# Second row tile normed first, stored values in their own pool, second half's sums in strips, short tile not last, idle flips ahead of the rows

## The chip, the cores and the metric

The kernel runs on one core of one Trainium2 chip. The metric is the device time of one execution in microseconds. Engines: TensorE (PE, its weight loads PEld), VectorE (DVE), ScalarE (ACT), GpSimd (POOL), and SyncE (SP), which issues nearly all DMAs from one queue in order.

## The reference

A two-layer encoder step, for a prompt of 2048 rows and a sample of 64 rows, model width 1024, 16 heads of 64. What matters here is the part ahead of each attention:

```
layer a: h = rms_norm(x, norm_a);  q, k, v, gate = split(h @ w_in_a, 4)
         band attention (own chunk of 64 and 8 before), * silu(gate), @ w_out_a, + x
shared:  h = rms_norm(x1, norm_kv); k, v = split(h @ w_kv, 2)
layer b: h = rms_norm(x1, norm_b);  q, gate = split(h @ w_in_b, 2)
         stick-breaking attention over k, v, * silu(gate), @ w_out_b, + x1
out:     rms_norm(x2, norm_f); k and v rows of both layers are outputs too
```

All in float32, with each product made of three products of high and low parts (h·h, h·l, l·h).

## The kernel before, in words

`projections` is called once per layer and does the part above. It has four stages, each for a half of the rows (half 0: rows 0 to 1023 and the 64 sample rows, half 1: rows 1024 to 2047):

1. **Values of half 0.** Row tiles of 128 are loaded (`fetched`), normed (`normed`: square on ACT, mean on DVE, power and scaling on POOL, or scaling on DVE where that is asked for), turned by eight 128x128 flips on PE (`turned`) and cut into high and low parts (`parted`, into x_own for half 0 and x_big for half 1). Then `values` makes v for one row tile and one half of the columns: 24 products on PE for a full tile, 16 for the sample tile (rows 2048 to 2111, tile 16). The weights of a column half come as four raw blocks (`block_rows`), cut into eight pairs vwh, vwl (`two_blocks`: ACT and DVE); the second column half's are written over the first's. `leave` evicts: a cuts v and stores it (vs), b copies it (vn), stores it twice, and puts off loading the row before each row (vps), a subtraction and a store (vs), by a count of ticks (`after`, `tick`). In b the last three tiles of the second column half leave their difference to staged work beside the pairs (`stage_diff`).
2. **Pairs of half 0.** The k, q and gate projections are made for two blocks of 128 columns at once by a Strassen-like scheme (`pair`): eight slots, each of 12 products into ps_x, ps_z or ps_y. Some products take sums and differences of quarters of the rows' forms (`mix`: one, two, three, for each of four column strips u) as moving operand (`mixed`), others differences of the weights (t1 to t4, made by `weights_of`: load, s1, s2 scale on POOL; b1, b2 cut whole forms; −t1 and so on subtract on POOL; t1 and so on cut). Slot 0 needs b1, then evicts to c on ACT and cuts t2; slot 1 needs t1 and the sums. Other work is staged beside the slots (`all_pairs`, `staging`).
3. **Values of half 1**, as 1. Its first tiles and weight blocks are prepared in the last pairs of half 0; the weight blocks of rows 512 and up lie in x_own, in the first four row groups and the columns below 512. The sums go to x_own too, which holds the forms of half 0 no more.
4. **Pairs of half 1** for the kinds that aren't left for the attention stage (8 pairs in a, 4 in b).

The order on each engine: while `order.on` is set, compute instructions stay in the order in which they are written; elsewhere a scheduler orders them by a simulated timeline. DMAs by `nc.sync` are ordered by it too, and SP issues them in order. Pools of tiles are stacked: a pool opened after another was closed takes its place in memory, and a tile's first writer waits for the accesses of what lay there. vs and vn were tiles of the values' pool (v0, v1), where the pairs' pool (st0, st1: t2 to t4, c, hl and others) comes next. After both layers' projections come their attention stages, which the change does not touch.

Of the kernel before, what the change touches and what calls it, by code (L numbers as in the profile page):

```python
# [44 lines left out]
RATE = dict(a=0.4, b=0.3)  # L45
LAG = dict(a=3, b=5)
# [78 lines left out]
def encoder_step(ctx: ExitStack, tc: tile.TileContext, a: dict, o: dict):  # L125
# [143 lines left out]
    def projections(L, x_of, begin, w_v, cv, gv, out_v, jobs, first, prompt, sample, stages):  # L269
        with ExitStack() as own, ExitStack() as beside, ExitStack() as early:  # L270
# [11 lines left out]

            def mixed(hf, i):

                if hf == 0 and i == 3:
                    return quarter(0, 0, 1)
                x, r = sums[hf][i // 2], 4 * (i % 2)
                return [lambda k, c=c: x[:, r + k, c : c + CH] for c in (0, CH)]

            def into(hf, i, u):  # L290
                if hf == 0 and i == 3:
                    return [x[:, :4, CH + u * P : CH + u * P + P] for x in xs[0]]
                x, r = sums[hf][i // 2], 4 * (i % 2)
                return [x[:, r : r + 4, c + u * P : c + u * P + P] for c in (0, CH)]
# [94 lines left out]
            waiting, flight, lagging, seqs = [], [], [], [[*range(NK), len(TOK) - 1], [*range(NK, 2 * NK)]]  # L389
# [15 lines left out]
            def values(hf, half, i, t, vws, pool, vps):  # L405
                r0, n = TOK[t]
# [22 lines left out]
                def leave():  # L429
# [17 lines left out]
                    if L == "a" or half and t in seqs[hf][-3:]:  # L447
                        return
# [74 lines left out]
            def pair(hf, kind, c0, hp, forms, pool, this, following, third, event):  # L523
# [9 lines left out]
                def plain(ps):  # L533
                    c = pool.tile([P, CH], F32, name="c", tag="c", bufs=CS[L])
                    act.activation(c, ps, AF.Copy)
                    return c
# [111 lines left out]
            def all_pairs(hf, todo, made, forms, pool, staging, events):  # L648

                for i, (kind, w, c0, g, hp) in enumerate(todo):  # L650

                    def event(p):
                        for x in events.get(i, {}).get(p, []):
                            x()
                        flight[:] = [x for x in flight if any(x[0] is y for y in waiting)]
                        left = max(8 * (staging["until"] - i) - p, 1)
                        staging["due"] += len(staging["todo"]) / left if staging["todo"] else 0
                        while staging["todo"] and staging["due"] >= 1:
                            tags, stage = staging["todo"][0]
                            if any(sum(tag in x[1] for x in flight) >= n for tag, n in tags.items()):  # L660
# [8 lines left out]
                    pair(hf, kind, c0, hp, forms, pool, made[i], following, third, event)  # L669
# [39 lines left out]
            with tc.tile_pool(name=f"v0_{L}", bufs=1) as pool:  # L709
# [17 lines left out]
                xt[1] = load(seq[1])  # L727
                tile1 = turned(seq[1], norm(seq[1], xt[1]))
# [7 lines left out]
                for i, t in enumerate(seq):  # L736
                    leave = values(0, 0, i, t, vws, pool, vps)
# [10 lines left out]
                    if i == len(seq) - 1:  # L748
                        vws = [x for j in range(4) for x in two_blocks(j, raw[j], vw(pool))]
                    leave()  # L750
                    if i >= 4:
                        mixing.pop(0)()
                    tick()
                for i, t in enumerate(seq):
                    values(0, 1, i, t, vws, pool, vps)()
# [7 lines left out]
                    if 4 <= i < 8:  # L763
                        split(*into(0, 3, i - 4), tmp[i].rearrange("p (k t) -> p k t", k=4))
# [24 lines left out]
            staging = dict(pool=spaces.__enter__(), todo=staged[0], until=last - 2, due=1.0)  # L789
# [41 lines left out]
            all_pairs(0, todo[0], made, forms, spool, staging, events)  # L831
# [6 lines left out]
            with tc.tile_pool(name=f"v1_{L}", bufs=1) as pool:  # L838
                vps = two_places() if L == "b" else None
                where = [(ahead, 2), (ahead, 2), (ahead, 2), (pool, 1), (ahead, 2), (ahead, 2), (pool, 1), (ahead, 2)]  # L840
                xt[3] = fetched(seq1[3], *where[3])
                for i, t in enumerate(seq1):
                    leave = values(1, 0, i, t, vws, pool, vps)
# [4 lines left out]
                    if i < 4 or L == "a" and i < 5:  # L848
                        values_beside(i, ("oh", "ol"))
                    if i == 5:  # L850
                        raw = [block_rows(1, j, ("xr", "xr", "oh", "oh")[j]) for j in range(4)]
                    if i == NK - 1:
                        vws = [x for j in range(4) for x in two_blocks(j, raw[j], vw(ahead if j < 2 else pool))]
                    leave()
                    if i + 3 < NK:
                        normed(seq1[i + 3], xt[i + 3], ahead)
                    if i == NK - 1:
# [4 lines left out]
                    tick()  # L862
                for i, t in enumerate(seq1):
                    values(1, 1, i, t, vws, pool, vps)()
                    for _ in range(1 + i % 2):
# [8 lines left out]
                    if i == 2:  # L874
                        run(made[0], "s1")
                    if i == 4:
# [8 lines left out]
                forms[1] = whole_forms("ol")  # L885
            early.close()
            spool = beside.enter_context(tc.tile_pool(name=f"st1_{L}", bufs=1))
# [5 lines left out]
            run(made[0], "b2", "-t2", "-t4")  # L893
            run(made[1], "load", "s1")
            all_pairs(1, todo[1], made, forms, spool, staging, {})
# [692 lines left out]
    new_diffs = [("new", t, 1) for t in (6, 7, 16, 13, 14, 15)]  # L1588
# [6 lines left out]
    staged_b = [new_diffs[0], keys_b[10], new_diffs[1], outs[0], new_diffs[2]]  # L1595
# [19 lines left out]
    with (  # L1615
# [173 lines left out]
        (beside_b, [staged_b, new_diffs[3:]]),  # L1789
# [287 lines left out]
```

## Time and profile before

| | us |
|---|---|
| median of 3 runs (lowest, highest) | 3258.44 (3257.12, 3260.55) |
| profiled execution, its own time | 3262.03 |
| its span, first to last instruction | 3260.2 |
| PE busy | 3142.9 (96%) |
| values of half 0 in a, first flips to the first pair | 7 to 125 |
| values of half 1 in a | 397 to 496 |
| values of half 0 in b | 1405 to 1525 |
| values of half 1 in b | 1808 to 1914 |

Of the granted clock, the mean over the span is 0.989 of full speed. In the timeline a row has start, duration, engine, line, operation, out<-in, sizes and count, and in brackets the idle time of the engine before it with its releaser. In the view by stretches a row has the stretch, its length, the busy time and count of PE, PEld, DVE, ACT and POOL, PE's granted clock, the DMA engines' share and GB/s. The chain of waits has start, duration and what. Line 114 is the helper through which every compute instruction is issued, so tiles' names tell the place. A tile keeps its name where its memory is used for something else: x_new holds t1 in the second half, bigl holds t1 and t2 in the first.

### The profile page before, as it was taken

What the parts mean: (1) busy time and instruction counts of PE and PEld (TensorE: products, weight loads), DVE (VectorE), ACT (ScalarE), POOL (GpSimd) and SP (SyncE); (2) the same over time, 40 slices, a digit from 0 to 9 for tenths busy, and PEclk for the clock granted to TensorE, in tenths of its full rate; (3) what the DMA queues carried; (4) which work ended last, traced back from release to release, by engine and by line L of the source; (5) the groups of instructions that cost most, each with busy time, mean ns of one, the idle gap of its engine ahead of it and who ended that gap; (6) DMA issues with size and microseconds to landing.
All of it is one profiled execution on the core that took longest, in us unless ns stands there. A gap on an engine that the chain in (4) does not pass through costs nothing.

```text
span 3260.2 us, 52067 instructions
## 1 busy us (share of the span) xinstructions
PE 3142.9 (96%) x16760; PEld 2625.2 (81%) x16760; DVE 2229.5 (68%) x3938; ACT 1861.9 (57%) x3743; POOL 1717.8 (53%) x2383
## 2 busy tenths in 40 slices
PE   8999999999998999998999989999999999999999
PEld 6787887778887898876888767888888888888877
DVE  5676456567777775256545563888878888888873
ACT  4344444558887775043544444666666666666662
POOL 3455347736665553024543262444467777777761
PEclk9999999999999999999999989999999999999999
DMA  6598547788899994467988867977835566355423
GB/s 211 180 334 296 177 182 248 259 248 233 225 272 248 249 238 134 149 230 237 302 316 301 274 216 234 251 208 199 220 112 150 148 199 192 115 146 142 137 72 120
DMA packets 476686, 684.74 MB, mean 210 GB/s; under 512 B 61137, under 2 KB 258289, under 8 KB 476414
## 3 DMA queue, kind: packets, MB, share of 16 engines
q1 hardware_dynamic: 474110, 673.03, 67.6%
q10 hardware_dynamic: 2304, 8.39, 0.7%
q8 instruction: 133, 2.18, 0.3%
q14 instruction: 139, 1.14, 0.1%
HBM read 422.54 MB, written 258.76 MB: 209 GB/s over the span
## 4 chain that ended last, share of the span: by engine, by line
PE 39%; DVE 6%; issue 3%; DMA 2%; ACT 1%; POOL 1%; SPq 0%; ACTq 0%; POOLq 0%; DVEq 0%
PE acc L114 7%; PE z L114 6%; PE wt L114 6%; PE ps_j L114 5%; PE ps_x L114 5%; PE ps_o L114 3%; PE ps_z L114 3%; DVE s L114 2%; DVE pl L114 2%; PE ps_v L114 1%; PE ps_y L114 1%; PE ps_q L114 1%; DMA kt<-k_b 0%; ACT ph L114 0%; PE ps_n L114 0%
## 5 line engine op out<-in xcount | busy, mean ns | idle before, releaser
L114 DVE TENSOR_TENSOR pl<-wt,ph 128x512 fp32r<-128x512 f32 (+1 forms) x864 | 551.1, 653 | 110.2 <-ACT ph L114 106.5
L114 ACT ACTIVATE ph<-wt 128x512 fp32r<-128x512 f32 (+1 forms) x864 | 485.1, 578 | 193.3 <-PE wt L114 180.9
L114 PE MATMUL wt<-ident,s 128*128 128x128 f32 x3472 | 552.6, 274 | 9.3 <-DVE pl L114 7.3
L114 PEld LDWEIGHTS wt<-ident,s 128*128 128x128 f32 x3472 | 418.5, 141 | 84.2 <-DVE pl L114 13.3
L114 ACT ACTIVATE f<-z 128x512 f32<-128x512 f32 (+4 forms) x680 | 355.1, 536 | 194.5 <-PE z L114 130.4
L114 POOL TENSOR_TENSOR s<-f,s 128x256 f32<-128x256 f32 x416 | 361.3, 869 | 104.0 <-DVE s L114 95.5
L114 PE MATMUL acc<-ph,vt 128*128 128x512 f32 (+3 forms) x1088 | 375.2, 379 | 6.9 <-DMA vt<-v_a 2.5
L114 PE MATMUL z<-kt,q 128*128 128x512 f32 (+3 forms) x1280 | 373.0, 378 | 5.3 <-ACT f L114 2.8
L114 PE MATMUL acc<-pl,vt 128*128 128x512 f32 (+3 forms) x1088 | 364.0, 368 | 9.3 <-DVE pl L114 8.9
L114 POOL TENSOR_TENSOR two<-f 128x256 f32<-128x256 f32 x416 | 260.2, 627 | 153.1 <-ACT f L114 141.5
L114 POOL TENSOR_SCALAR s<-s,rc 128x640 f32<-128x640 f32 (+5 forms) x264 | 202.1, 771 | 241.2 <-DVE rc L114 173.0
L114 DVE TENSOR_TENSOR_SCAN s<-two,s,own 128x256 f32<-128x256 f32 x408 | 299.8, 737 | 33.8 <-POOL two L114 32.5
L114 PEld LDWEIGHTS z<-kt,q 128*128 128x128 f32 x1280 | 220.3, 190 | 36.0 <-ACT f L114 10.4
L114 DVE CUSTOM_DVE_ANT_0 s<-z,bias 128x640 f32<-128x640 f32 (+4 forms) x256 | 184.5, 732 | 70.6 <-PE wt L114 53.7
L114 PEld LDWEIGHTS acc<-pl,vt 128*128 128x128 f32 x1088 | 193.9, 190 | 43.0 <-DVE pl L114 27.5
L114 PE MATMUL ps_x<-x_own,t 128*128 128x512 f32 x864 | 219.4, 402 | 6.3 <-ACT t L114 2.3
L114 POOL TENSOR_TENSOR wraw<-wraw 128x512 f32<-128x512 f32 x96 | 136.5, 1430 | 168.4 <-DVE ohl L114 85.1
L114 DVE TENSOR_TENSOR_SCAN s<-f,own 128x128 f32<-128x128 f32 (+4 forms) x264 | 202.3, 787 | 30.5 <-ACT f L114 30.0
L114 PEld LDWEIGHTS acc<-ph,vt 128*128 128x128 f32 x1088 | 197.0, 190 | 29.6 <-ACT ph L114 8.9
L114 POOL TENSOR_TENSOR rstd<-ms,nhalf 128x1 f32<-128x1 f32 (+1 forms) x51 | 33.8, 662 | 347.1 <-DVE ms L114 340.3
L114 PE MATMUL ps_o<-big,oh 128*128 128x512 f32 x544 | 213.7, 393 | 0.0
L114 ACT ACTIVATE s<-s,mn 128x640 f32<-128x640 f32 (+5 forms) x264 | 200.3, 760 | 23.0 <-DVE mn L114 22.1
(248 smaller groups left out, 7336.9 us busy)
## 6 DMA issues: line engine op xcount, KB each, us to landing
vt<-v_b SPq DMA_DIRECT2D x80, 512.0 KB, 4.9
v_b<-vs SPq DMA_DIRECT2D x64, 512.0 KB, 4.1
q<-q_a SPq DMA_DIRECT2D x128, 256.0 KB, 5.0
q<-q_b SPq DMA_DIRECT2D x128, 256.0 KB, 4.2
vt<-v_a SPq DMA_DIRECT2D x48, 512.0 KB, 7.4
kt<-k_b SPq DMA_DIRECT2D x96, 256.0 KB, 5.7
v_a<-vs SPq DMA_DIRECT2D x40, 512.0 KB, 2.9
keys<-k_a SPq DMA_DIRECT2D x80, 256.0 KB, 7.0
```

The lines of the kernel that those rows point to most:

```text
L114: ins = op(*args, **kwargs)
```

## The change

It does these things:

- In the first stage, the first two row tiles are loaded and normed (scaling on DVE) before the first weight blocks are cut; before, the second was loaded and normed behind two pairs of them, with the scaling on POOL. In b this second norm is outside the written order.
- In a, 24 flips of the identity into an unused bank stand ahead of the first row tile on PE.
- The sample tile is second to last in half 0, not last. The tick of the second to last tile of the first column half comes in the last tile, behind the second half's weight blocks and before the eviction. The mixing steps start one tile earlier.
- vs and vn have pools of their own (v0s, v1s), above v0 and v1. The pairs' pool of half 1 is two pools: one for t2, the raw weights and c, and one for the rest.
- In b, the last four tiles of the second column half (before: three) leave their difference to staged work: tiles 5 and 12 are new there.
- In half 1 the sums lie in strips: strip u has the row groups and column half (u//2, u%2), so that three of four don't touch the weight blocks. Their order is 1, 2, 3, 0; mixing starts at the fourth tile of the first column half (before: at its last) and is done two tiles earlier; the weights' steps move forward by one to three tiles, and b2, −t2 and −t4 stand beside the values.
- In half 1 the fourth tile (index 3) is loaded into a buffer of the tag ol; w_out parts and differences that use ol there use xr.
- The second pair's s1 is in slot 0 of the first pair; staged work of half 0 starts one item later.

```diff
+COLD = 24
+            def strips(i):
+                x = x_own[i // 2].rearrange("p (r k) (h j c) -> p r k h j c", r=2, h=2, j=4)
+                return [x[:, :, :, :, i % 2 * 2 + j] for j in range(2)]
...
             def into(hf, i, u):
...
+                if hf:
+                    return [x[:, u // 2, :, u % 2] for x in strips(i)]
...
-[[*range(NK), len(TOK) - 1], [*range(NK, 2 * NK)]]
+[[*range(NK - 1), len(TOK) - 1, NK - 1], [*range(NK, 2 * NK)]]
...
-                    if L == "a" or half and t in seqs[hf][-3:]:
+                    if L == "a" or half and t in seqs[hf][-4:]:
...
             def times(ps, x, w, begin):
+                if len(x[0](0).shape) > 2:
+                    ps = ps.rearrange("p (r h c) -> p r h c", r=2, h=2)
...
-            with tc.tile_pool(name=f"v0_{L}", bufs=1) as pool:
+            with tc.tile_pool(name=f"v0_{L}", bufs=1) as pool, tc.tile_pool(name=f"v0s_{L}", bufs=1) as vspool:
...
-                xt = {0: load(seq[0])}
-                if L == "b":
-                    norm(seq[0], xt[0], scale=dve.tensor_scalar)
+                xt = {i: load(seq[i]) for i in range(2)}
+                order.on = L == "a"
+                if L == "a":
+                    cold = bank("cold")
+                    for _ in range(COLD):
+                        flip(cold[:, :P], ident)
+                for i in range(2):
+                    norm(seq[i], xt[i], scale=dve.tensor_scalar)
+                    if i == 0:
+                        order.on = True
+                        tile0 = turned(seq[0], xt[0])
+                        order.on = L == "a"
                 order.on = True
-                if L == "a":
-                    norm(seq[0], xt[0], scale=dve.tensor_scalar)
-                tile0 = turned(seq[0], xt[0])
...
-                xt[1] = load(seq[1])
-                tile1 = turned(seq[1], norm(seq[1], xt[1]))
+                tile1 = turned(seq[1], xt[1])
...
                     if i == len(seq) - 1:
                         vws = [x for j in range(4) for x in two_blocks(j, raw[j], vw(pool))]
+                        tick()
                     leave()
-                    if i >= 4:
+                    if 3 <= i < len(seq) - 1:
                         mixing.pop(0)()
-                    tick()
+                    if i != len(seq) - 2:
+                        tick()
...
+                where = [(ahead, 2), (ahead, 2), (ahead, 2), (Strip(), 2), (ahead, 2), (ahead, 2), (pool, 1), (ahead, 2)]
...
-                        values_beside(i, ("oh", "ol"))
+                        values_beside(i, ("oh", "xr"))
...
-                        mixing = [x for u in range(4) for x in mix(1, u, tmp)]
+                        mixing = [x for u in (1, 2, 3, 0) for x in mix(1, u, tmp)]
+                    if 3 <= i < NK - 1:
                         mixing.pop(0)()
...
-                    for _ in range(1 + i % 2):
+                    for _ in range(1 + (i in (0, 2))):
...
+                    if i == 3:
+                        run(made[0], "b1", "s2")
                     if i == 4:
-                        run(made[0], "b1", "s2")
+                        run(made[0], "-t1")
+                    if i == 5:
+                        run(made[0], "t1")
                     if i == 6:
-                        run(made[0], "-t1")
+                        forms[1] = whole_forms("ol")
+                        run(made[0], "b2")
                     if i == 7:
-                        run(made[0], "t1")
+                        run(made[0], "-t2", "-t4")
...
-            forms[2] += [spool.tile([P, 2, 4, P], F32R, name=f"t{i}", tag=f"t{i}", bufs=1) for i in (2, 3, 4)]
+            forms[2] += [spool.tile([P, 2, 4, P], F32R, name="t2", tag="t2", bufs=1)]
...
+            rest = beside.enter_context(tc.tile_pool(name=f"st1b_{L}", bufs=1))
+            forms[2] += [rest.tile([P, 2, 4, P], F32R, name=f"t{i}", tag=f"t{i}", bufs=1) for i in (3, 4)]
...
-    new_diffs = [("new", t, 1) for t in (6, 7, 16, 13, 14, 15)]
+    new_diffs = [("new", t, 1) for t in (5, 6, 7, 16, 12, 13, 14, 15)]
```

More of the change, by code (lines that the diff above doesn't have):

```diff
@@ L286, in mixed @@
                     return quarter(0, 0, 1)
+                if hf:
+                    return [lambda k, x=x: x[:, :, k] for x in strips(i)]
                 x, r = sums[hf][i // 2], 4 * (i % 2)
@@ L521, in times, with pair @@
                     mm(ps, w[1](k), x[0](k), start=False, stop=(k == 3), skip_group_check=True)
-            def pair(hf, kind, c0, hp, forms, pool, this, following, third, event):
+            def pair(hf, kind, c0, hp, forms, pools, this, following, third, event):
+                cpool, pool = pools
                 r0 = HALVES[hf][0]
@@ L533, in plain @@
                 def plain(ps):
-                    c = pool.tile([P, CH], F32, name="c", tag="c", bufs=CS[L])
+                    c = cpool.tile([P, CH], F32, name="c", tag="c", bufs=CS[L])
                     act.activation(c, ps, AF.Copy)
@@ L646, in pair, with all_pairs @@
                     lagged()
-            def all_pairs(hf, todo, made, forms, pool, staging, events):
+            def all_pairs(hf, todo, made, forms, pools, staging, events):
                 for i, (kind, w, c0, g, hp) in enumerate(todo):
@@ L668, in all_pairs @@
                     following, third = ([*made[i + 1 :], {}, {}])[:2]
-                    pair(hf, kind, c0, hp, forms, pool, made[i], following, third, event)
+                    pair(hf, kind, c0, hp, forms, pools, made[i], following, third, event)
             def slot(x):
@@ L736, in projections @@
                 for i, t in enumerate(seq):
-                    leave = values(0, 0, i, t, vws, pool, vps)
+                    leave = values(0, 0, i, t, vws, vspool, vps)
                     if i + 4 < len(seq):
@@ L749, in projections @@
                         vws = [x for j in range(4) for x in two_blocks(j, raw[j], vw(pool))]
+                        tick()
                     leave()
-                    if i >= 4:
+                    if 3 <= i < len(seq) - 1:
                         mixing.pop(0)()
-                    tick()
+                    if i != len(seq) - 2:
+                        tick()
                 for i, t in enumerate(seq):
-                    values(0, 1, i, t, vws, pool, vps)()
+                    values(0, 1, i, t, vws, vspool, vps)()
                     if mixing:
@@ L762, in projections @@
                         run(made[0], "load")
-                    if 4 <= i < 8:
-                        split(*into(0, 3, i - 4), tmp[i].rearrange("p (k t) -> p k t", k=4))
+                    if 4 <= t < 8:
+                        split(*into(0, 3, t - 4), tmp[t].rearrange("p (k t) -> p k t", k=4))
                     if i == 3:
@@ L788, in projections @@
             last, next_vws, next_xt, got = len(todo[0]) - 1, [], {}, {}
-            staging = dict(pool=spaces.__enter__(), todo=staged[0], until=last - 2, due=1.0)
+            staging = dict(pool=spaces.__enter__(), todo=staged[0], until=last - 2, due=0.0)
             def begin_next():
@@ L830, in projections @@
             }
-            all_pairs(0, todo[0], made, forms, spool, staging, events)
+            all_pairs(0, todo[0], made, forms, (spool, spool), staging, events)
             while waiting:
@@ L837, in projections, with tile @@
             ahead, vws, xt = got["pool"], next_vws, next_xt
-            with tc.tile_pool(name=f"v1_{L}", bufs=1) as pool:
+            with tc.tile_pool(name=f"v1_{L}", bufs=1) as pool, tc.tile_pool(name=f"v1s_{L}", bufs=1) as vspool:
                 vps = two_places() if L == "b" else None
-                where = [(ahead, 2), (ahead, 2), (ahead, 2), (pool, 1), (ahead, 2), (ahead, 2), (pool, 1), (ahead, 2)]
+                class Strip:
+                    def tile(self, shape, dtype, name, tag, bufs):
+                        return opool.tile(shape, dtype, name=name, tag="ol", bufs=2)
+                where = [(ahead, 2), (ahead, 2), (ahead, 2), (Strip(), 2), (ahead, 2), (ahead, 2), (pool, 1), (ahead, 2)]
                 xt[3] = fetched(seq1[3], *where[3])
                 for i, t in enumerate(seq1):
-                    leave = values(1, 0, i, t, vws, pool, vps)
+                    leave = values(1, 0, i, t, vws, vspool, vps)
                     if i + 4 < NK:
@@ L856, in projections @@
                         normed(seq1[i + 3], xt[i + 3], ahead)
-                    if i == NK - 1:
+                    if i == 3:
                         tmp = [opool.tile([P, 2, CH], F32, name="mixed", tag="ol", bufs=2) for _ in range(2)]
                         tmp = [x[:, j] for x in tmp for j in range(2)]
-                        mixing = [x for u in range(4) for x in mix(1, u, tmp)]
+                        mixing = [x for u in (1, 2, 3, 0) for x in mix(1, u, tmp)]
+                    if 3 <= i < NK - 1:
                         mixing.pop(0)()
-                    tick()
+                    if i != NK - 2:
+                        tick()
                 for i, t in enumerate(seq1):
-                    values(1, 1, i, t, vws, pool, vps)()
-                    for _ in range(1 + i % 2):
+                    values(1, 1, i, t, vws, vspool, vps)()
+                    for _ in range(1 + (i in (0, 2))):
                         if mixing:
@@ L892, in projections @@
             staging["pool"] = beside.enter_context(tc.tile_pool(name=f"s1_{L}", bufs=2))
-            run(made[0], "b2", "-t2", "-t4")
-            run(made[1], "load", "s1")
-            all_pairs(1, todo[1], made, forms, spool, staging, {})
+            run(made[1], "load")
+            all_pairs(1, todo[1], made, forms, (spool, rest), staging, {0: {0: [partial(run, made[1], "s1")]}})
             assert not staged[1]
```

13 lines of the change are left out of this document (8 added, 5 removed).

## The prediction, made before the changed kernel was built or run

> **What bounds the kernel now.** I read the page's first part, then what TensorE (PE) waited for, by stretches.
>
> ```profile
> span 3260.2 us, 52067 instructions
> PE 3142.9 (96%) x16760; PEld 2625.2 (81%) x16760; DVE 2229.5 (68%) x3938; ACT 1861.9 (57%) x3743; POOL 1717.8 (53%) x2383
> ```
>
> PE is busy 3142.9 of 3260.2 us, so time is gained where PE stands still or runs slow. The waits of PE (total, times, longest), first in layer a, 0 to 135 us and 390 to 520 us:
>
> ```profile
> PE ps_v L114 <- DVE vwl L114: 1.3, 2, 0.7
> PE ps_x L114 <- ACT bigl L114: 1.3, 1, 1.3
> ```
> ```profile
> PE ps_z L114 <- ACT x_new L114: 5.9, 1, 5.9
> ```
>
> then in layer b, 1320 to 1540 us and 1815 to 1940 us:
>
> ```profile
> PE ps_x L114 <- ACT bigl L114: 8.7, 1, 8.7
> PE ps_tr L114 <- POOL xt L114: 5.4, 1, 5.4
> PE ps_v L114 <- ACT vwh L114: 4.3, 1, 4.3
> ```
> ```profile
> PE ps_z L114 <- ACT x_new L114: 10.8, 1, 10.8
> PE ps_tr L114 <- POOL xt L114: 2.1, 1, 2.1
> PE ps_x L114 <- ACT t L114: 1.4, 1, 1.4
> ```
>
> All of them lie in the function `projections`, called once per layer, which is nearly all that the change edits. A wait costs twice. Behind it the granted clock (the column after POOL's) is half:
>
> ```profile
> 504.40:508.50 4.10, 4.02 (x10) 3.06 (x11) 2.06 (x3) 1.87 (x4) 1.64 (x2) 0.50 0.78 254
> ...
> 1474.40:1477.90 3.50, 3.37 (x8) 2.69 (x9) 3.50 (x7) 3.50 (x6) 0.00 (x0) 0.51 1.01 379
> 1539.30:1542.70 3.40, 3.37 (x8) 2.65 (x9) 1.38 (x2) 0.98 (x2) 0.00 (x0) 0.50 0.80 261
> 1829.10:1832.90 3.80, 3.74 (x14) 3.25 (x15) 1.45 (x3) 2.56 (x5) 0.01 (x1) 0.55 0.43 105
> 1926.90:1931.90 5.00, 4.89 (x12) 3.69 (x12) 3.38 (x5) 1.64 (x3) 0.47 (x1) 0.51 0.25 105
> 1935.20:1938.70 3.50, 3.50 (x10) 2.73 (x9) 0.24 (x1) 0.00 (x0) 2.66 (x5) 0.51 0.45 158
> ```
>
> PE works at half rate there, so about half of its busy time in such a row is lost: 2.0, 1.7, 1.7, 1.7 (3.74 at a share of 0.55), 2.4 and 1.7 us. I now give each part of the change the wait that it touches.
>
> **Second row tile first, layer a.** The timeline of ACT, of DVE, of POOL and of PE, and the DMA rate at the start (last column, GB/s):
>
> ```profile
> 7.24 1.34 ACT L114 ACTIVATE vwh<-vraw,g_a 128x512 fp32r<-128x512 f32 x2 [2.00 <-DMA vraw<-in_w_in_a]
> ```
> ```profile
> 10.80 1.05 ACT L114 ACTIVATE junk<-xt 128x1024 bf16<-128x1024 f32 x1
> ```
> ```profile
> 17.62 1.42 DVE L114 SCALAR_TENSOR_TENSOR vwl<-vraw,g_a,vwh 128x512 fp32r<-128x512 f32 x2
> ```
> ```profile
> 20.16 1.12 POOL L114 TENSOR_SCALAR xt<-xt,rstd 128x1024 f32<-128x1024 f32 x1
> ```
> ```profile
> 23.68 1.03 PE L114 MATMUL ps_tr<-ident,xt 128*128 128x128 f32 x8
> ```
> ```profile
> 0.00:20.00 20.00, 7.59 (x26) 6.32 (x27) 10.37 (x17) 11.78 (x19) 3.80 (x11) 1.00 0.88 285
> ```
>
> The second tile's square (10.80) stands behind four weight blocks and the first tile's eviction on ACT; so its flips and all products start late, and the third tile's flips, which follow the first tile's products on PE, come at 23.68. Moved ahead, the second load goes in front of the weights: 512 KB at 285 GB/s are 1.8 us, less some overlap, so vwh starts at about 8.9, not 7.24. From its first result (9.6) DVE has eight vwl of 0.71 and four evictions, which I count as long: 8.4 us, so the last vwl is done at 18.0 instead of 19.04. PE no longer decides; DVE does. From the last vwl to POOL's scaling of the third tile it was 1.1 us (19.04 to 20.16), and the scaling takes 1.1; so the third tile's flips come at 20.2 instead of 23.68: **3.5 us gained**. Bounds: 2 (the weights land later than I think) and 5.5 (DVE keeps up and PE alone decides).
>
> The 24 idle flips cost nothing: identity is ready by 1.3, and at the cold price of eight flips, 1.97 us (a row of layer b below), they end at 7.2, about when the first tile's flips can start; what those feed waits for ACT until after 10. Uncovered they would cost at most their own 5.9. What they gain hangs on the clock. Eight flips take 1.97 or 1.04 us in the rows below, so flips run at the granted clock; that flips alone raise it, no row shows. The Trainium skill ("TensorE: Matmul & The Clock Gate", Part 4: PE-mode transpose) says that transposes don't count as PE activity for the full rate. By that rule the flips buy nothing and the first tile's products end, as an estimate, at 19.4; without it at 18.6. Both are ahead of 20.2, so the term is 0 either way.
>
> **Second row tile first, layer b.**
>
> ```profile
> 1411.17 1.97 PE L114 MATMUL ps_tr<-ident,xt 128*128 128x128 f32 x8 [5.37 <-POOL xt L114]
> ...
> 1420.13 1.04 PE L114 MATMUL ps_tr<-ident,xt 128*128 128x128 f32 x8
> ```
> ```profile
> 1396.75 8.85 SPq L372 DMA_DIRECT2D vraw<-in_w_kv  x4
> ```
>
> Here the norms are not held in the written order and can move under the last output products; the second tile's flips would follow the first's at 1405.8 (1411.17 − 5.37). What is late next: the last of these weight loads is issued at 1405.6, which puts the last vwl near 1413.3, and the third tile's flips 2.2 later, 1415.5 instead of 1420.13: **4.6 gained**. Bounds 2.5 (the norm stays behind) and 7.7 (PE alone: 1405.8 and 1.0 of flips and 5.6 of products).
>
> **Short tile not last, ticks behind the blocks.** Between the column halves the second half's weights are written over the first's.
>
> ```profile
> 1472.45 0.63 ACT L114 ACTIVATE vs<-vps 128x512 fp32r<-128x512 f32 x1 [2.24 <-issue]
> 1472.99 5.00 ACT L114 ACTIVATE vwh<-vraw,g_kv 128x512 fp32r<-128x512 f32 x8
> ```
> ```profile
> 72.62 6.85 DVE L114 SCALAR_TENSOR_TENSOR vwl<-vraw,g_a,vwh 128x512 fp32r<-128x512 f32 x8
> ```
>
> In b the blocks (1472.99) queue behind difference steps whose loads are late. The change emits the blocks first, and gives them a full tile as cover: 24 products of 0.23 us are 5.5 us against 5.0 of ACT; the short tile has 16, 3.7 us. The wait of 4.3 and its 1.7 of clock go; a late first vwl remains, which I put at 0.5: **5.5** (3.5 to 6.0). In a it is DVE that is late (6.85 for eight), and a mixing step still stands ahead of it: **0.5** of 1.3 (0 to 1.3).
>
> **Stored values in their own pool.** Into the pairs of the first half, the chain of waits in b and ACT's timeline in a:
>
> ```profile
> 1532.72 5.13 DMA v_b<-vs
> ```
> ```profile
> 129.26 0.60 ACT L114 ACTIVATE c<-ps_x 128x512 f32<-128x512 f32 x1 [3.67 <-DMA v_a<-vs]
> ```
>
> The next pool's tile c lies where vs was, so ACT waits for the last store (5.13 us in b); behind c on ACT stands t2, written to bigl, for which PE waits 8.7 in b and 1.3 in a. With vs and vn above, the next pool (34 KB per partition: t3, four c, four hl and small ones) fits under the 46 KB of row tiles and weight blocks, whose last reader is PE itself. One more difference step per half goes to the staged ones, so none is left at the end. Gain 8.7 + 1.7 + 1.3 = **11.7** (7 to 11.7). The two staged differences (tiles 5 and 12) add two loads of 256 KB, a POOL subtraction and a split each, during pairs in which PE is busy without a gap; uncovered, ACT's and DVE's parts are some 1.3 us each.
>
> **Third tile of the second half in the strip buffer.**
>
> ```profile
> 1817.01 4.89 DMA q_b<-hl
> ```
>
> This xt lay over hl; its issue waited for hl's store, and SP's queue with it, and the tile came 2.1 us late. Its new place is free once the last pair's weights have been read, before that store. 2.1 and 1.7 of clock go, and some is left: **3.7** (1.5 to 3.8). The same page of the Trainium skill (section "Why this matters for your kernels") allows gaps up to about 3 us; this gap of 2.05 us was followed by the half clock, so the measurement decides. By the page the term would be 2.1.
>
> **Sums in strips, mixed sooner.** Into the pairs of the second half of b:
>
> ```profile
> 1926.35 0.61 ACT L114 ACTIVATE x_new<-wraw 128x512 fp32r<-128x512 f32 x1
> ...
> 1932.50 0.60 ACT L114 ACTIVATE c<-ps_x 128x512 f32<-128x512 f32 x1 [2.48 <-DMA v_b<-vs]
> ```
>
> PE stops at 1916 (it starts again at 1926.9, 10.8 later) for t1 (x_new), cut at 1926.35 at the end of a queue of mixing, differences and stores on ACT and DVE. The change runs four of the twelve mixing steps in the first column half (now one), ends them two tiles earlier, cuts t1 two tiles earlier, and b2 and two differences before the values end. Two tiles are 11 us, as much as the lag of 10.8. Then c (1932.50): its part of the pool (t2, raws, c: 20 KB) lies over one xt and eight weight blocks, no longer over stores. Gone are 10.8 + 2.4 and 1.4 + 1.7, together 16.3; I leave 1.3 for a new short wait: **15** (8 to 16.3). In a the same wait is 5.9 with 2.0 of clock: **7.9** (4 to 7.9).
>
> With strips a product's moving operand comes in four runs of 128. The nearest row has runs of 128 with 256 columns (ps_q), against 512 in one run:
>
> ```profile
> 1543.91 1.87 PE ps_q L114 x16
> 1545.78 2.74 PE ps_z L114 x12
> ```
>
> 0.117 us for 256 columns and 0.228 for 512: the runs cost nothing.
>
> **Sum.** In a 3.5 + 0.5 + 7.9, in b 4.6 + 5.5 + 3.7 + 15, in both 11.7: 52.4 us. The profiled execution took 3262.0 us (span 3260.2 and 1.8 around it), 3.6 above the median of 3258.4. So a profiled one would take 3209.6, and the median **3206**. The low ends sum to 28.5, the high ends to 60.
>
> **Rivals.** (1) *The sums stay late*, since DVE and POOL bound that stage, whatever the order:
>
> ```profile
> 1900.00:1920.00 20.00, 16.24 (x71) 12.89 (x69) 16.68 (x18) 7.24 (x12) 17.00 (x15) 0.95 0.60 203
> ```
>
> For it: 16.68 and 17.00 of 20 us busy just before PE stops. Against: three steps leave this half, and its last two tiles get only weights. Half of 15 + 7.9 would come back: 3217. (2) *The pools don't do what they say*: the first tile of a new pool still waits for everything stored before. Then 11.7 and the 3.1 behind c are missing: 3221; both, 3232. For it: it is the tile allocation that decides, which no trace shows; against: the sizes above. (3) *Slower*: the strips. If each run of 128 cost as much as a flip of 128 does (1.04 us for 8, 0.13 each), a mixed product would take 0.52 us instead of 0.228. The second halves have 12 pairs with 48 mixed products, 576: +168 us, 3374. It decides from 0.09 us more per product on (52.4 / 576). The ps_q row speaks against it.
>
> **How the numbers follow.** Forecast 0.62, (1) 0.15, (2) 0.12, both 0.04, (3) 0.03; 0.04 for gains eaten elsewhere, no change. The range of 8 in 10 goes from 3196, near the high ends (3198), to 3234, both rivals. A measurement can't tell less than 0.2%, 6.5 us, from no change; with that, faster 0.92, same 0.04, slower 0.04.
>
> **What would show it.** In the waits of PE, x_new and bigl gone or under 2 us each, ps_v after vwh gone, ps_tr after POOL xt under 3 in sum; no half clock near 505, 1475, 1540, 1830 and 1927 (less what was gained by then); the third tile's flips at 20 us; twelve products over the sums still in 2.74. I am wrong if c still names a store as its releaser, if t1 is still cut after the last product of the values, or if a product over the strips takes more than 0.24 us.

## The result, and the profile after

The changed kernel takes 3227.14 us (median of 4 runs, 3225.53 to 3228.30) against 3259.49 for the kernel before (the three runs of the table above and a fourth): a ratio of 0.9896, 95% interval 0.9877 to 0.9914. The forecast was 3206, the range 3196 to 3234. So it is faster, by about 32 us instead of 52. In the traces, too, the two spans differ by 35.0.

The page's first part for the changed kernel:

```profile
span 3225.2 us, 52124 instructions
PE 3141.7 (97%) x16784; PEld 2620.3 (81%) x16784; DVE 2220.1 (69%) x3938; ACT 1862.7 (58%) x3743; POOL 1711.0 (53%) x2383
```

PE's idle time fell from 117.3 to 83.5 us (span less busy). Its busy time, which contains what the half clock costs, fell by 1.2. The 24 new idle flips are 4.7 of it, so that of the work common to both fell by 5.9; the prediction had counted 11.2 for the clock. Before, the two largest waits of the first stretch were these, which the list in the prediction leaves out:

```profile
PE ps_tr L114 <- DVE xt L114: 7.0, 1, 7.0
PE ps_tr L114 <- POOL xt L114: 5.4, 1, 5.4
```

What PE waited for after the change, in the same four stretches as before (0 to 135, 390 to 520, 1320 to 1540, 1815 to 1940 us; total, times, longest):

```profile
PE ps_tr L115 <- DVE x_own L115: 1.6, 1, 1.6
PE ps_tr L115 <- DVE xt L115: 1.4, 2, 0.8
...
PE ps_tr L115 <- POOL xt L115: 1.1, 1, 1.1
```
```profile
PE ps_x L115 <- ACT t L115: 1.2, 1, 1.2
PE ps_v L115 <- DVE vwl L115: 1.1, 3, 0.7
```
```profile
PE ps_f L115 <- DVE nn L115: 2.5, 1, 2.5
PE ps_tr L115 <- POOL xt L115: 2.0, 2, 1.5
PE ps_v L115 <- ACT x_own L115: 1.6, 1, 1.6
PE ps_v L115 <- DVE x_own L115: 1.6, 1, 1.6
```
```profile
PE ps_x L115 <- ACT t L115: 3.7, 2, 3.4
PE ps_v L115 <- DVE vwl L115: 1.1, 3, 0.7
PE ps_v L115 <- ACT vwh L115: 0.8, 1, 0.8
```

x_new (5.9 and 10.8 before) is gone, bigl went from 8.7 to 0.4. New are nn and x_own, and where t1 was late the wait for the next form, t, grew from 1.4 to 3.7. The half clock stands behind three waits in b, and in a pair near 250 us, where it had not been; the granted clock is the column after POOL's:

```profile
254.40:257.80 3.40, 3.40 (x10) 2.63 (x9) 3.28 (x9) 1.90 (x4) 0.00 (x0) 0.50 0.91 353
1452.50:1455.90 3.40, 3.26 (x8) 2.58 (x9) 2.66 (x6) 1.22 (x2) 0.00 (x0) 0.51 0.86 260
1524.20:1530.90 6.70, 6.36 (x18) 4.97 (x19) 2.79 (x5) 1.95 (x4) 4.64 (x8) 0.50 0.73 230
1899.60:1906.40 6.80, 5.71 (x13) 4.09 (x14) 1.72 (x2) 1.53 (x4) 6.20 (x10) 0.50 0.96 369
```

At half rate that is 9.4 us lost, against 11.2 in the rows of before. One row of before was not among those, the start of b:

```profile
1411.10:1416.40 5.30, 5.23 (x17) 4.45 (x18) 3.43 (x6) 3.45 (x6) 0.11 (x2) 0.50 0.95 358
```

Its loss, 2.6 us, is gone, as part of the gain at that start. The next table takes the start of the same PE instruction in both traces and says by how much the lead grew in each place:

| place | predicted | measured |
|---|---|---|
| a, start | 3.5 | 5.2 |
| a, column halves of the first half | 0.5 | 1.4 |
| a, into the first half's pairs (own pool) | 1.3 | 2.2 |
| a, near 250 us, in a pair | 0 | −3.2 |
| a, column halves of the second half | 0 | −2.2 |
| a, into the second half's pairs (sums) | 7.9 | 6.4 |
| b, start | 4.6 | 4.8 |
| b, column halves of the first half | 5.5 | 0.7 |
| b, into the first half's pairs (own pool) | 10.4 | 4.9 |
| b, third tile of the second half | 3.7 | 3.4 |
| b, column halves of the second half | 0 | −3.2 |
| b, into the second half's pairs (sums) | 15 | 9.8 |
| elsewhere | 0 | 5.0, of it 3.6 in the attention of b |

### The profile page after: what moved, and what is told of

It is laid out like the page before. It is cut to its first block, busy times and chain, and to the rows that moved or that the text cites. A ratio compares the mean times of both kernels' runs of the same rounds, so it can differ in the third digit from the quotient of the medians.

```text
span 3225.2 us, 52124 instructions
## 1 busy us (share of the span) xinstructions
PE 3141.7 (97%) x16784; PEld 2620.3 (81%) x16784; DVE 2220.1 (69%) x3938; ACT 1862.7 (58%) x3743; POOL 1711.0 (53%) x2383
## 5 line engine op out<-in xcount | busy, mean ns | idle before, releaser
L115 PE MATMUL ps_o<-bigl,oh 128*128 128x512 f32 x544 | 213.0, 392 | 0.0
```

The costliest lines, as they stand in the source:

```text
L115: ins = op(*args, **kwargs)
```

## The experiments

Places are read with the same table, against the changed kernel. Two profiles of one kernel (e10 and e12) ended 2.6 us apart in it and differed by 2.9 at one place, so a difference under 3 at one place says little unless the wait itself moved. The edits are shown shortened.

**The idle flips.** `COLD = 24` became 0.

> The changed kernel without its 24 idle flips at the start; everything else as changed. Theory A (flips alone raise the granted clock, and PE, not DVE, decides the start): in the changed kernel the first tile's eight flips took 1.09 us and its products ran from 10.75 to 17.29 at full rate, with the third tile's flips at 18.43 behind POOL's scaling. Without the idle flips the first tile's flips take 1.97 again and the products lose 1.9 to half clock, end near 19.2, and the third tile's flips start there: 0.8 us later, and 0.8 us more at the end. Theory B (the prediction's: nothing hangs on them, since something else decides): third tile's flips at 18.4, 0 us. Theory C (flips don't raise the clock, it came from something else): products as fast as now, 0 us.

Measured 3227.95, 0.8 more, within the spread. In the trace the start lost 1.2. PE's timelines, changed kernel and then without flips:

```profile
1.34 4.70 PE L115 MATMUL cold<-ident 128*128 128x128 f32 x24 [1.34 <-POOL ident masks.py:199]
6.88 1.09 PE L115 MATMUL ps_tr<-ident,xt 128*128 128x128 f32 x8 [0.84 <-DVE xt L115]
...
18.43 1.09 PE L115 MATMUL ps_tr<-ident,xt 128*128 128x128 f32 x8 [1.14 <-POOL xt L115]
```
```profile
7.00 2.82 PE L115 MATMUL ps_tr<-ident,xt 128*128 128x128 f32 x12 [7.00 <-DVE ms L115]
```

Eight flips take 1.09 us after the idle ones, and twelve take 2.82 without them (0.14 against 0.24 each). Nothing but flips had run, so flips do raise the clock: A for the clock. All twelve profiles with the idle flips agree, with 1.09 to 1.16 for the first eight. (The column of the granted clock can't show it; it reads 1.00 from 6 to 9 us in e1, too.) But the gaps behind the first flips take the clock away again: in eight of the twelve it is half for 3.4 us from about 11 us on (0.50 from 11.6 to 15.0 in e6), though not in that of the changed kernel. Those eight are 0.1 to 0.9 later at the start than the changed kernel, so the flips buy 0.3 to 1.2 us, which the time doesn't resolve.

**The short tile's place.** First the old order everywhere (e2), then only in the second column half (e6):

```
-seqs = [[*range(NK - 1), len(TOK) - 1, NK - 1], ...]
+seqs = [[*range(NK), len(TOK) - 1], ...]                                  # e2
-for i, t in enumerate(seq):  values(0, 1, ...)
+for i, t in enumerate([*range(NK), len(TOK) - 1]):  values(0, 1, ...)     # e6
```

> The changed kernel with the short tile put last again in the first half; the ticks, pools and sums stay as changed. Theory A (the tile that follows the short one has only its 16 products, 3.7 us, as cover for its own eviction, and it is now the tile whose split and whose stored sums end the half, so the loads of the second pair's weights go out 5.5 us later): in layer b the waits for x_own at the halves (3.2 us, and 1.7 of half clock) go, the first new block is waited for about 1.3 us instead, and the wait for nn in the first pair (2.48 us and 3.4 of clock) goes as well: 3 to 8 us faster, 3219 to 3224. Theory B (the prediction's: the full tile as cover of the weight blocks is most of the 5.5 us at the halves of b): PE waits 3 to 4 us for vwh or vwl there, and the time is 3 to 5 us longer, 3230 to 3232.

> The changed kernel with the short tile last in the second column half of the first half alone; in the first column half it stays last but one. Theory A: of the 5 to 7 us that the old order of tiles brings, the part at the first pair comes from the second column half: the last sums' split stands one tile earlier, so the second pair's weights are loaded some 5 us earlier, and the wait for nn (2.48 us, and half clock behind it) goes: 4 to 5 us faster at that place, while the waits for x_own between the column halves (1.64 and 1.56 us) stay. 3222 to 3223.5. Theory B: the loads wait for something else than that split (their place in SP's queue, the DMAs' load), and the wait for nn stays: 3226 to 3228.

e2 took 3221.41 (0.9884, 0.9869 to 0.9899): at the halves of b 1.3 better than the changed kernel, into the pairs 4.3 more. e6 took 3226.82, but gained 5.3 into the pairs of b; it lost as much in small pieces elsewhere, one of them a half clock twice as long near 254 us. Its time alone would fit B. In both the wait for nn is gone. ACT and POOL of the changed kernel there, then POOL of e6:

```profile
1512.46 0.62 ACT L115 ACTIVATE x_own<-bigl 128x512 fp32r<-128x512 f32 x1
1512.98 0.59 ACT L115 ACTIVATE c<-ps_x 128x512 f32<-128x512 f32 x1
...
1522.74 0.63 ACT L115 ACTIVATE t<-wraw 128x512 fp32r<-128x512 f32 x1 [4.66 <-POOL wraw L115]
1523.40 0.38 ACT L115 ACTIVATE nn<-ps_q 64x256 f32<-64x256 f32 x1
```
```profile
1519.64 1.84 POOL L115 TENSOR_SCALAR bigl<-bigl,g_kv 128x256 f32<-128x256 f32 x4 [9.52 <-DMA bigl<-in_w_kv]
1521.44 1.27 POOL L115 TENSOR_TENSOR wraw<-wraw 128x512 f32<-128x512 f32 x1
```
```profile
1520.56 2.39 POOL L115 TENSOR_SCALAR bigl<-bigl,g_kv 128x256 f32<-128x256 f32 x4 [5.23 <-DMA bigl<-in_w_kv]
1522.92 1.29 POOL L115 TENSOR_TENSOR wraw<-wraw 128x512 f32<-128x512 f32 x1
```

c no longer waits for a store. But the buffer of the second pair's weights holds tile 7's sums until x_own<-bigl (1512.46), since tile 7 comes last; its load is late, POOL stands 9.5 us at the scaling, and the difference behind it (1521.44) holds t, and t holds nn. PE of e6 is 5.2 us later up to there; against PE, its scaling starts 4.3 earlier and its difference 3.7. So A holds, in both runs. Not separated is how much the load's place in SP's queue has to do with it: it stands behind stores of the last tiles' values, which moved along.

The waits for x_own stayed in e6, as A said. ACT and DVE of the changed kernel at the halves of b:

```profile
1448.66 0.63 ACT L115 ACTIVATE vs<-vps 128x512 fp32r<-128x512 f32 x1 [3.05 <-DVE vps L115]
1449.20 0.61 ACT L115 ACTIVATE vs<-woraw 128x512 fp32r<-128x512 f32 x1
1449.72 1.06 ACT L115 ACTIVATE x_own<-ps_tr 128x512 fp32r<-128x512 f32 x2
```
```profile
1446.85 1.78 DVE L115 TENSOR_TENSOR vps<-vps,vn 128x512 f32<-128x512 f32 x1
1449.32 0.98 DVE L115 TENSOR_TENSOR vs<-vps,vs 128x512 fp32r<-128x512 f32 x1 [0.70 <-ACT vs L115]
1450.22 1.76 DVE L115 TENSOR_TENSOR vs<-woraw,vs 128x512 fp32r<-128x512 f32 x1
1451.91 1.28 DVE L115 TENSOR_TENSOR x_own<-ps_tr,x_own 128x512 fp32r<-128x512 f32 x2
```

The last tile's eviction stands behind a difference step and a split of w_out, with the short tile's 3.7 us as its only cover.

**The stored values' own pool.** The pool split undone, at all four calls:

```
-values(hf, half, i, t, vws, vspool, vps)
+values(hf, half, i, t, vws, pool, vps)
```

> The changed kernel with the stored values (vs, vn) back in the pool of the row tiles and weight blocks; nothing else undone. Theory A (the pools do what the change says): c stands behind a store of vs again in both layers, the wait of PE for bigl comes back with 5 to 9 us in b and 1 to 2 in a, the wait for nn behind it is absorbed, and c of the second half in b waits for a store too: 6 to 10 us slower, 3233 to 3237. Theory B (rival 2 of the prediction, the pools change nothing and the gain at that place came from elsewhere): within 2 us of 3227.

Measured 3236.52, 9.4 more (0.9929, 0.9913 to 0.9946). ACT in b, first and second half:

```profile
1523.26 0.60 ACT L115 ACTIVATE c<-ps_x 128x512 f32<-128x512 f32 x1 [4.33 <-DMA out_b_v_p<-vn]
```
```profile
1910.85 0.60 ACT L115 ACTIVATE c<-ps_x 128x512 f32<-128x512 f32 x1 [4.56 <-DMA out_b_v_p<-vn]
```

A: c waits for stores again. But of the 9.4 only 0.9 and 0.5 fall into the pairs of the first half, where the prediction had put all 11.7; in b the wait for bigl (5.0) merely takes the place of the one for nn. 3.9 in a and 3.4 in b fall into the second half.

**The mixing.** The second half's mixing moved whole into its second column half (e4); then only its last early step (e9).

```
-if 3 <= i < NK - 1:  mixing.pop(0)()        # e4: gone;      e9: 3 <= i < NK - 2
-for _ in range(1 + (i in (0, 2))): ...      # e4: range(2);  e9: range(1 + (i < 3))
```

> The changed kernel with all twelve mixing steps of the second half in its second column half, two at each of the first six tiles; strips, t1, b2 and the differences of the weights stay where the change put them. Theory A (mixing on POOL and DVE in the first column half delays the weight blocks there, and without it the sums come late): the losses of the changed kernel at the halves of the second half (3.2 us in b, 2.2 in a) go, but x_new is waited for again, 4 to 8 us in b and 2 to 4 in a with clock behind it: 1 to 7 us slower, 3228 to 3234. Theory B (only the order of t1 and b2 decides, not how much is mixed when): the losses go and nothing comes back: 3221 to 3223. Theory C (those losses have nothing to do with mixing): they stay, and the sums come late on top: 3233 to 3240.

> The changed kernel with no mixing step at the last tile but one of the second half's first column half (POOL's 7.1 us of adding that run beside the weight blocks); that step goes to the second column half, two steps at each of the first three tiles. Theory B (POOL's adding stretches DVE's steps): in b the waits for vwh and vwl (0.77 and 0.69 us, with some small ones) go, 2 to 3 us gained at that place; in a, where a product of the blocks is waited for too, 2.2 gained as in the run that mixed late. Theory A (the order, not POOL's speed): under 1 us in b, the 2.2 in a. For both the sums come one step later, 1 to 3 us lost in each layer: A 3226 to 3230, B 3223 to 3227.

e4: 3243.30, 16 more, outside all three ranges. The waits of PE into the second half's pairs, in a and in b:

```profile
PE ps_z L115 <- ACT x_new L115: 4.0, 1, 4.0
```
```profile
PE ps_z L115 <- ACT x_new L115: 7.1, 1, 7.1
PE ps_x L115 <- ACT t L115: 3.2, 1, 3.2
PE ps_v L115 <- ACT vwh L115: 2.5, 1, 2.5
```

The early start is worth 8.0 in a and 7.7 in b at that place; in a that is twice what theory A had. The loss at the halves of a came back (2.2): there it is the mixing. In b it did not. e9: 3235.57, 8.4 more, outside both ranges; 3.9 are lost at the sums of a, 0.2 in b, nothing is gained at the halves, and the rest lies at places that the edit doesn't touch. It could not tell what it was meant to: POOL takes the moved step up as early as before, since nothing else stands ahead of it. POOL of the changed kernel and of e9, beside the new blocks:

```profile
1839.41 7.12 POOL L115 TENSOR_TENSOR mixed<-big,bigl 128x512 f32<-128x512 f32 x6 [6.39 <-DVE mixed L115]
```
```profile
1848.76 7.12 POOL L115 TENSOR_TENSOR mixed<-big,bigl 128x512 f32<-128x512 f32 x6 [6.39 <-DVE mixed L115]
```

**Staging, buffers of the blocks, b2.** Three edits in three places (e5):

```
-staging = dict(..., due=0.0)
+staging = dict(..., due=float(L == "a"))
-block_rows(1, j, ("xr", "xr", "oh", "oh")[j])
+block_rows(1, j, ("oh", "oh", "xr", "xr")[j])
 # second half: b2 at tile 5 (was 6), -t2 and -t4 at tile 6 (was 7)
```

> The changed kernel with three small edits, each in a stage of its own, so that each is read at its own place in the trace. (i) In layer a the staged work starts with one step due at once, as before the change. Theory A: the 3.6 us lost near 250 us come from where the staged cache loads now fall, and return. Theory B: they come from the stores of that stretch whatever the staging, and stay. (ii) The new weight blocks of the second half's second column half lie in the other order of buffers, the first two where w_out's raw rows were, not where its split parts wait for their store. Theory A: the third block's load, issued at 1841.05 behind that store and landed at 1847, comes earlier, and 1.5 to 3 of the 3.2 us lost there in b return. Theory B (mixing on DVE and POOL makes the blocks late): 0 to 0.5. (iii) In the second half b2 and the last two differences of the first weights stand one tile earlier. Theory A (the order alone makes t2 late): the wait for t, 3.44 us in b with half clock behind it and 1.6 us in a, goes: 5 in b and 1.5 in a gained. Theory B (DVE and ACT are full up to there, and what is moved ahead makes t1 or x_new as late): 0 to 2 in b. All A: 3213 to 3217. All B: 3224 to 3227.

3226.69 in all, in the range for all B. (i) A in part: PE's wait near 250 us fell from 3.85 to 2.26 and 1.6 came back; the half clock stayed. (ii) 0.8 came back: the blocks run without a break now, but the first is as late. (iii) B: in a 2.9 was lost, in b 0.3 gained. ACT of the changed kernel in b, and of e5:

```profile
1898.52 0.63 ACT L115 ACTIVATE vs<-vps 128x512 fp32r<-128x512 f32 x1 [1.89 <-DVE vps L115]
1899.06 0.58 ACT L115 ACTIVATE vn<-ps_v 128x512 f32<-128x512 f32 x1
1899.53 0.59 ACT L115 ACTIVATE c<-ps_x 128x512 f32<-128x512 f32 x1
1900.01 0.63 ACT L115 ACTIVATE t<-wraw 128x512 fp32r<-128x512 f32 x1
```
```profile
1901.63 0.59 ACT L115 ACTIVATE c<-ps_x 128x512 f32<-128x512 f32 x1
1902.10 0.63 ACT L115 ACTIVATE t<-wraw 128x512 fp32r<-128x512 f32 x1
```

t stands behind the last difference step, vn and c on ACT; moving b2 alone didn't help it (PE's wait for t is 4.2 in e5).

**Difference step and mixing exchanged** at the last tile but two (e8):

```
-mixing.pop(0)();  tick()
+tick();  mixing.pop(0)()
```

> The changed kernel with one pair of steps exchanged in each first column half: at the last tile but two, the due difference step (less, and its split) is written ahead of the mixing step instead of behind it. Theory A (the blocks at the column halves are late because ACT waits for vs<-vps, which DVE does only behind the mixing step: 3.1 us of ACT's time in the second half of b): the first new block is started 2 to 3 us earlier there, and 2 to 3 of the 3.2 us lost at that place return; in the first half of b the eviction x_own stands less far behind, 1 to 2 us. 3222 to 3225. Theory B (not the order, but POOL's mixing, which runs at the same time and stretches DVE's steps from 0.68 to 1.78 us): under 1 us at either place, 3226 to 3228. Theory C (the difference step's load is not there any earlier, so that DVE only waits in another place and the mixing is late on top): 0 to 2 us slower at the sums, 3227 to 3230.

3234.44, 7.3 more, outside all three ranges. A has the first step right and not its result: the first block of the second half in b comes in time, but the third waits for its raw rows (PE's wait for vwh 3.7, ACT's 6.2), and 4.3 are lost. In the first half of b nothing changed.

**Together.** e7 has the edits of e5 and e6 and the short tile fifth. e10 has the short tile last in b, the three edits of e5 (b2 in b only), and the difference of tile 11 staged as well; e12 is e10 again; e11 adds an earlier eviction of the short tile, and e8's exchange in the second half.

```
+seqs = [[*range(4), len(TOK) - 1, *range(4, NK)], ...]                         # e7
+seqs = [[*range(NK), len(TOK) - 1] if L == "b" else ..., ...]                  # e10, e11, e12
+if L == "a" or half and t in (5, 6, 7, 16, 11, 12, 13, 14, 15):  return        # e10, e11, e12
+new_diffs = [("new", t, 1) for t in (5, 6, 7, 16, 11, 12, 13, 14, 15)]         # e10, e11, e12
+if L == "b" and i == len(seq) - 3:  tick()    # e11: behind parted(), not at the end of the tile before
```

> All edits of the two runs before together, and the short tile fifth in the first column half. Theory A (the waits for x_own between the column halves come from the many steps queued there, of which few stand behind the fifth tile): these 3.2 us and the 1.7 of clock behind them go as well, and the full tile covers the weight blocks: 3204 to 3208. Theory B (whatever tile follows the short one, its eviction has too little cover): a wait of 1.5 to 3 us for x_own with half clock behind it appears at the sixth tile, near 1430 us: 3208 to 3213.

> The changed kernel with: the short tile last in both column halves in b alone; the staged work of a starting at once; the raw blocks of the second half in the other order of buffers; in b one more difference (tile 11) moved from the values to the staged work, and b2 and the last two differences of the weights one tile earlier, in b alone. Theory A (t is late in b because ACT and DVE take the last difference step, the last vn and c ahead of it, and without that step it comes about 2 us sooner): the wait for t at the first pair of the second half in b goes from 3.4 to under 1.5 us and its half clock to 3.4 us or none, 3 to 5 gained there; with 5 to 6.5 at the end of the first half of b, 1.6 near 250 us and 0.8 at the halves: 3213 to 3217. Theory B (that wait comes from POOL's subtraction, done only behind b2, whatever stands on ACT): it stays at 3 us or more, 3218 to 3221.

> The kernel of e10 with two exchanges. In the first half of b the eviction of the short tile is written ahead of the difference step and the split of w_out's rows that stood before it, so that the last tile's products don't wait. In the second half the due difference step is written ahead of the last mixing step but one, as in e8, now with the raw blocks in the other order of buffers. Theory A (these evictions and blocks are late because of their place in the queues of ACT and DVE): the wait of 2.02 us for x_new at the column halves of b goes, and its half clock with it, 2 to 5 us; the first new block of the second half is no longer waited for, and the load that cost e8 3.7 us is early enough in the other buffer, 1 to 3 us: 3 to 8 us faster than e10, whose median was 3217.5. Theory B (DVE is so full there, with its steps stretched to 1.78 us beside POOL's adding, that the waits only move to the blocks behind): within 2 us of e10.

> The kernel of e10 once more, beside e11 on the same chip, so that the two can be compared: 3215 to 3220, and its profile shows how much of the places where nothing was changed (the attention stages, the clock behind equal gaps) differs from one run to the next. Theory A of e11 puts e11 3 to 8 us below it, theory B within 2 us.

e7: 3223.11, outside both theories; the x_own waits went, a wait for xt of 2.0 with half clock came at the same halves. e10: 3217.45 (0.9869, 0.9854 to 0.9884), just above A's range. e12: 3216.39 (0.9853, 0.9838 to 0.9868). This version beats both kernels by its times.

At the sums of b, A has the first step right and misses the next. The wait of 3.4 for t is gone in e10, and 1.3 of it is left in e12. But two slots on, where the changed kernel waits 0.2 for the next t, both wait 2.3. ACT of e10 there:

```profile
1897.89 0.63 ACT L115 ACTIVATE t<-wraw 128x512 fp32r<-128x512 f32 x1 [5.81 <-POOL vvp L115]
```

vvp is a difference that was staged: by the profile this t is released only behind POOL's subtraction of that difference. So the place gains 4.2 in e10, where no half clock follows, and 1.2 in e12, where 3.4 us of it do. Steadier are 4.2 in both into the pairs of the first half of b, and 1.3 at its halves; e2 has both, so they come from the order of the tiles.

e11: 3220.05, 3.7 slower than e12 on the same chip, outside both theories, though the intervals overlap (0.9851 to 0.9884). It gained nothing, as B said: in the first half x_new is no longer waited for, and vwh is, for 1.9; in the second the raw rows now come in time, but vwl is waited for, 1.4 in five pieces.

## Why the prediction was right, and where it was off

The sign and the range held, and most waits went for the reasons given. Two steps failed, one term was too large, three losses were not priced, and the sum was 20 us too good by the times, 17 by the traces. That the range holds the result is in part luck: it reached to 3234 for the two rivals together, one of which fell, while the losses came from elsewhere, and 3.6 of the gain lie where nothing was changed. Of the signs, x_new, bigl, c and t1 came out as said; the waits for POOL's xt sum to 3.9, not under 3, and the half clock stands again at three of the five places named.

- **Starts, third tile.** Right. In a DVE decided, as said, and POOL's scaling after it (PE waits 1.1 for it); 5.2 instead of 3.5 because vwh began at 7.9, not 8.9. The flips' term, 0, is not refuted by the time; in the traces it is 0.3 to 1.2, since DVE was done earlier than reckoned, and so PE's clock counts after all.
- **Column halves of b, 5.5: measured 0.7.** The failed step is "gives them a full tile as cover". The cover was taken from the last tile's own eviction, which the prediction never priced. e2, e7 and e11 show one wait of about 2 us in each order, at another tensor.
- **Own pool in b, 10.4: measured 4.9.** The wait for the store went (e3), and up to the products behind it the lead grew by 9.9; then about 5 were lost again at nn and its half clock. What failed is taking all of bigl's 8.7 as gain: the prediction asked where the stall goes, but not what the new order of tiles does to the next pair's load, which shares a buffer with the last tile's sums. e6 shows 5.3 for this.
- **Sums, 15 and 7.9: measured 9.8 and 6.4.** t1 is in time. What is late next is t2; the 1.3 left for "a new short wait" had to be 3.4 and a half clock of 6.8. Of what the prediction booked here, the part behind c belongs to the pool (3.4 in b by e3).
- **Not priced at all:** the four mixing steps in the first column half (2.2 in a by e4), the staging that starts later in a (1.6 by e5). The 3.2 at the second half's column halves of b is settled in part: 0.8 is the order of buffers; that the rest is the first block behind vs<-vps is argued, not shown, since e8 starts that block in time and ends worse.
- **Clock.** Six stretches of half clock were booked as gains, 11.2 us; four came back elsewhere, 9.4. PE's busy time fell all the same, since both starts lost their half clock as well (2.6 in b; in a the first eight flips take 1.09 instead of 1.97).
- **Rivals.** (1) is half true: what DVE, ACT and POOL do there stays late, but for t2, not t1. (2) fell with e3. (3) fell in one line of PE's timeline, before and after, 12 products over the sums in b:

```profile
1954.25 3.02 PE L114 MATMUL ps_z<-x_own,x_new 128*128 128x512 f32 x12
```
```profile
1943.94 3.02 PE L115 MATMUL ps_z<-x_own,x_new 128*128 128x512 f32 x12
```

Open are the 3.6 us in the attention of b, where nothing was changed. Against the changed kernel, other profiles moved there by −2.7 (e1) to 2.0 us (e12), so some of it may be no effect at all. 2.3 of it arise at one spot, near 2680 us in the trace of before: there PE waits 1.25 (0.20 after) and the clock is half for 3.4 us (0.50; 1.00 after).

## What to carry to other kernels

When a stall goes, follow the next two instructions on every engine that stood behind it, and count what the new order takes from others: cover, buffers, queue places. Book the idle time of a wait as gain, but the half clock behind it only as likely as the new waits are few: here 9.4 of 11.2 us came back. A transition in which two engines were full kept about one wait in every order tried. Exchanging work there (b2 in e5, e8, e11) gained nothing, and taking work out (e10's staged difference) removed one wait and made another two slots on.

## What the runs showed of the hardware

**Half clock is a lottery in fixed pieces.** Inside the spans here it lasted 3.41 us or a multiple: 6.83, 10.24 or 13.65 (the last in the kernel before, 1918.2 to 1931.8 us). Two runs of one kernel, each right behind a wait of 1.47 us:

```profile
1403.00:1406.40 3.40, 3.38 (x19) 2.92 (x20) 1.44 (x3) 2.61 (x5) 0.29 (x1) 1.00 0.68 211
```
```profile
1403.40:1406.80 3.40, 3.40 (x13) 3.01 (x13) 1.38 (x2) 2.22 (x5) 0.00 (x0) 0.51 0.47 146
```

So the same gap costs 1.7 us in one run and nothing in the next. The Trainium skill ("TensorE: Matmul & The Clock Gate", Part 1) describes a free-running activity window of about 3.4 us; these rows agree. Its Part 4 says that transposes don't engage the full rate; eight flips in 1.09 us after nothing but flips (e1 beside the changed kernel) speak against it, so here the measurement decides.

**DVE is slow beside POOL.** A subtraction of two tiles in SBUF takes 0.68 us, and 1.78 (the row at 1446.85) while POOL adds:

```profile
1445.10 6.34 POOL L115 TENSOR_TENSOR bigl<-x_own,x_own 128x512 f32<-128x512 f32 x4 [1.29 <-DVE bigl L115]
```

e9 could not move POOL's adding, but the changed kernel's trace of b has 25 such subtractions of full tiles (vps<-vps,vn). The eleven with POOL idle take 0.68 or 0.69, three beside POOL's scaling 0.68 to 0.88, and of seven beside this adding six take 1.77 or 1.78 and one 1.23. No other of the 25 takes more than 0.69. So the slow ones go with POOL's adding. The Trainium skill ("GPSIMD Engine Reference", 1. Specifications) names contention for such DVE instructions with two SBUF inputs, which fits.
